# Finer steps at the sub-layer boundaries of a two-layer hybrid trunk: the last residual block in halves, and the second token tile's normalised blocks in a new order on ScalarE and VectorE

## The chip, the cores and the metric

The kernel runs on one core of one Trainium2 chip. A time is the device time of one execution in microseconds (us); lower is better. The kernel before took 1308.61 us, the median of 3 runs (1308.53 to 1309.16).

The core's engines each have an instruction queue that runs in order: PE (TensorE, the matrix engine), DVE (VectorE), ACT (ScalarE), POOL (GpSimd) and SP (SyncE, which issues most DMAs). An instruction can wait for a semaphore that another engine or a DMA raises; all that is queued behind it on its engine waits too.

## The reference, cut to what matters

256 tokens of width 1024 pass two layers. Each layer is an FFN, a mixer of four attention kinds, and a second FFN. Each sub-layer ends in a residual sum and a layer norm, and the next one begins with a modulation that is different in each:

```
for l in range(2):
    mod = (silu(c) @ ada_w[l] + ada_b[l]).reshape(-1, 3, 3, 1024)   # shift, scale, gate of each sub-layer
    h = 0.5 * swiglu(modulate(x, mod[0,0], mod[0,1]), w_in[l,0], w_out[l,0])
    x = layer_norm(ALPHA * x + (1 + mod[0,2]) * h, g[l,0], b[l,0])
    h = mixer(modulate(x, mod[1,0], mod[1,1]), ...)
    x = layer_norm(ALPHA * x + (1 + mod[1,2]) * h, g[l,1], b[l,1])
    h = 0.5 * swiglu(modulate(x, mod[2,0], mod[2,1]), w_in[l,1], w_out[l,1])
    x = layer_norm(ALPHA * x + (1 + mod[2,2]) * h, g[l,2], b[l,2])

modulate(x, shift, scale) = x * (1 + scale) + shift
swiglu(u, w_in, w_out)    = (silu(u @ w_in[:, :2816]) * (u @ w_in[:, 2816:])) @ w_out
```

## The kernel before, in words

**Split matmuls.** A float32 product is made of three matmuls. Each operand is split into a rounded high part (`hi`, made by ACT, line 262) and a low part that is the difference (`lo`, made by DVE, line 267); `split_mm` issues high by high, low by high and high by low (L286 to L288 where the weight is the stationary operand, L290 to L292 where the tokens are). The activations that a sub-layer reads are `uh` and `ul`, turned, with the width on the partitions; its weights stream in by DMA and are split as they come.

**Tiles.** The 256 tokens are two tiles, t=0 and t=1, of 128 partitions. A sub-layer's output is 2 x 1024 columns in four PSUM banks `accs`, each 128 x 512. In an FFN the hidden width of 2816 is 22 blocks of 128: `hidden(f)` makes one block, `post` its activation, `split_h` its two parts `hh` and `hl`, and `down` adds it to the four banks.

**The boundary.** There are five boundaries from one sub-layer to the next: FFN to mixer (first and fourth), mixer to FFN (second and fifth), FFN to FFN (third), and one end of the program. At each, the last matmuls run bank by bank in the order of `TAIL`, so the banks of t=0 end first and are normalised while PE is still at those of t=1. For each tile:
- `resid` (L401 to L403, DVE, one bank of 512 columns at a time): the sum times the gate row into `rt`, then ALPHA times x plus it, then `bn_stats`.
- `stats` (L406 and L407 on DVE, L408 on POOL): mean, variance, and the power -0.5 of it into `rstd`.
- `xhat` (four quarters q of 256 columns): normalised in place. The table `XA` says which quarters of each tile go to ACT (L416, with one small DVE instruction before them, L415); the rest go to DVE (L418). Before, tile 0 has two quarters on ACT and tile 1 none.
- `norm` (four quarters): PE turns two 128 x 128 blocks j into a PSUM bank (L426); ACT (L432) or DVE (L434) applies scale and shift into `utmp`; ACT casts it to `uh` (L436); DVE makes `ul = utmp - uh` (L437).

`GT` names, for each quarter of tile 0, behind which of the last matmuls its PE transposes are issued; `GF` and `GM` do so for tile 1, counted in contraction steps of the next sub-layer.

**What follows.** The next sub-layer's first matmuls use t=0 alone and run while t=1 is normalised: in an FFN the first two hidden blocks (a step kt of the contraction has two products, one of each block), in a mixer a piece of the V projection. Then the same matmuls run for t=1, in order of kt, so that quarter 0 is needed first. In an FFN, `h` of these first blocks stands with tokens on the partitions (L604, L605, L607) and is turned by PE (L609, `hT`) before it is split. Then `hidden(2)` and the rest follow. The affine part of the layer norm (`affine`, L485 and L486, four pieces of two DVE instructions) is needed only by the next residual sum and is issued in the hidden loop. A scheduler reorders by priority: work of a boundary is ahead (`tc.high_priority`), and `tc.issue_after(i)` holds an instruction behind another one in the order of issue.

## Time and profile before

| | |
|---|---|
| median of 3 runs | 1308.61 us |
| the profiled execution | 1315.82 us |
| its span (first to last instruction) | 1314.0 us |
| PE busy | 1265.7 us, 96% |
| DVE busy | 1036.5 us, 79% |
| ACT busy | 652.6 us, 50% |
| POOL busy | 142.8 us, 11% |
| granted TensorE clock | 0.998 of full speed |
| DMA, mean over the span | 229 GB/s |

A profile page sums a single execution of the program; it is 7.2 us longer than the median of the runs that were timed without a profile. Busy times of one engine can't be added to those of another, since the engines run beside each other. A row of the timeline gives the start and the duration of an instruction (or of `xN` that follow each other without a gap), and in brackets how long its engine had been idle and whose result ended that. Matmuls overlap: their pitch from start to start, not their duration, is the time that each costs PE. The places at which PE is idle are few, and those at the five boundaries are where the lines above meet.

### The profile page before, as it was taken

What the parts mean: (1) busy time and instruction counts of PE and PEld (TensorE: products, weight loads), DVE (VectorE), ACT (ScalarE), POOL (GpSimd) and SP (SyncE); (2) the same over time, 40 slices, a digit from 0 to 9 for tenths busy, and PEclk for the clock granted to TensorE, in tenths of its full rate; (3) what the DMA queues carried; (4) which work ended last, traced back from release to release, by engine and by line L of the source; (5) the groups of instructions that cost most, each with busy time, mean ns of one, the idle gap of its engine ahead of it and who ended that gap; (6) DMA issues with size and microseconds to landing.
All of it is one profiled execution on the core that took longest, in us unless ns stands there. A gap on an engine that the chain in (4) does not pass through costs nothing.

```text
span 1314.0 us, 23415 instructions
## 1 busy us (share of the span) xinstructions
PE 1265.7 (96%) x9178; PEld 1175.6 (89%) x9178; DVE 1036.5 (79%) x1701; ACT 652.6 (50%) x1023; POOL 142.8 (11%) x150
## 2 busy tenths in 40 slices
PE   6999999999999999999999999999999999999997
PEld 5989888989989889998989999899989898899995
DVE  7788887888786799877698877688878768976565
ACT  4554355447564554444355444354666545554440
POOL 0130000214222000000000000012060210100000
PEclk9999999999999999999999999999999999999999
DMA  9889893756665639887548987457476655585530
GB/s 341 324 285 313 302 306 141 255 185 223 225 235 181 227 127 319 302 277 262 175 147 312 311 282 248 128 171 239 163 248 232 222 182 175 215 315 193 187 135 33
DMA packets 85847, 300.42 MB, mean 229 GB/s; under 512 B 10604, under 2 KB 12316, under 8 KB 85736
## 3 DMA queue, kind: packets, MB, share of 16 engines
q1 hardware_dynamic: 84392, 298.00, 66.3%
q8 instruction: 72, 1.18, 0.4%
q10 hardware_dynamic: 576, 0.60, 0.1%
q0 software_dynamic: 768, 0.32, 0.1%
q14 instruction: 39, 0.32, 0.1%
HBM read 297.81 MB, written 1.07 MB: 227 GB/s over the span
## 4 chain that ended last, share of the span: by engine, by line
PE 43%; issue 19%; DMA 16%; DVE 15%; ACT 5%; POOL 1%; DVEq 0%; ACTq 0%; SPq 0%; POOLq 0%
PE mm L286 9%; PE mm L287 8%; PE mm L288 8%; DVE lo L267 6%; DMA raw<-in_w_in_dram 5%; DMA raw<-in_adac_dram 5%; PE acc L290 3%; PE acc L292 3%; PE acc L291 3%; ACT hi L262 3%; DMA raw<-in_w_out_dram 3%; DVE raw L308 3%; DMA raw<-in_mpair_dram 1%; PE tp L286 1%; PE mm L290 1%
## 5 line engine op out<-in xcount | busy, mean ns | idle before, releaser
L267 DVE TENSOR_TENSOR lo<-raw,hi 128x1024 fp32r<-128x1024 f32 (+2 forms) x421 | 508.1, 1222 | 161.3 <-ACT hi L262 159.2
L262 ACT CAST hi<-raw 128x1024 fp32r<-128x1024 f32 (+1 forms) x422 | 433.8, 1040 | 322.3 <-PE mm L287 126.9
L286 PE MATMUL mm<-uh,hi 128*128 128x256 f32 x2032 | 574.7, 283 | 5.3 <-DVE h L525 3.1
L287 PE MATMUL mm<-ul,hi 128*128 128x256 f32 x2032 | 571.2, 281 | 0.0
L288 PE MATMUL mm<-uh,lo 128*128 128x256 f32 x2032 | 570.6, 281 | 0.0
L286 PEld LDWEIGHTS mm<-uh,hi 128*128 128x128 f32 x2032 | 383.0, 189 | 12.2 <-issue 5.3
L287 PEld LDWEIGHTS mm<-ul,hi 128*128 128x128 f32 x2032 | 383.5, 189 | 1.3
L288 PEld LDWEIGHTS mm<-uh,lo 128*128 128x128 f32 x2032 | 383.1, 189 | 0.3
L308 DVE CUSTOM_DVE_ANT_0 raw<-raw,cond_row,adab 128x1024 f32<-128x1024 f32 x128 | 163.9, 1292 | 47.1 <-DMA raw<-in_adac_dram 47.0
L290 PE MATMUL acc<-hi,hh 128*128 128x512 f32 x352 | 140.6, 400 | 2.2 <-ACT hh L531 1.7
L291 PE MATMUL acc<-lo,hh 128*128 128x512 f32 x352 | 139.1, 395 | 0.8 <-DVE lo L267 0.8
L292 PE MATMUL acc<-hi,hl 128*128 128x512 f32 x352 | 137.6, 396 | 0.1
L290 PEld LDWEIGHTS acc<-hi,hh 128*128 128x128 f32 x352 | 66.1, 188 | 17.7 <-ACT hh L531 3.3
L531 ACT CAST hh<-h 128x256 fp32r<-128x256 f32 x82 | 33.2, 405 | 97.4 <-DVE h L525 95.7
L292 PEld LDWEIGHTS acc<-hi,hl 128*128 128x128 f32 x352 | 65.9, 187 | 17.1 <-DVE hl L532 0.6
L291 PEld LDWEIGHTS acc<-lo,hh 128*128 128x128 f32 x352 | 66.1, 188 | 15.0 <-DVE lo L267 1.1
L408 POOL TENSOR_TENSOR rstd<-rstd,nhalf 128x1 f32<-128x1 f32 x12 | 7.6, 634 | 479.8 <-DVE rstd L407 479.8
L532 DVE TENSOR_TENSOR hl<-h,hh 128x256 fp32r<-128x256 f32 x74 | 31.2, 421 | 12.6 <-ACT hh L531 12.6
L290 PE MATMUL acc<-hi,uh 128*128 128x256 f32 (+1 forms) x128 | 38.7, 303 | 1.5 <-ACT uh L436 1.4
L1073 POOL TENSOR_TENSOR merged<-merged,tg 128x512 f32<-128x512 f32 x16 | 24.8, 1548 | 135.7 <-DVE tg L1071 57.2
L286 PE MATMUL tp<-y,hi 128*128 128x256 f32 x112 | 33.2, 297 | 5.8 <-ACT pt L753 5.7
L292 PE MATMUL acc<-hi,ul 128*128 128x256 f32 (+1 forms) x128 | 38.3, 299 | 0.0
(242 smaller groups left out, 1519.7 us busy)
## 6 DMA issues: line engine op xcount, KB each, us to landing
raw<-in_w_in_dram SPq DMA_DIRECT2D x174, 512.0 KB, 5.5
raw<-in_adac_dram SPq DMA_DIRECT2D x128, 512.0 KB, 5.4
raw<-in_mpair_dram SPq DMA_DIRECT2D x104, 512.0 KB, 4.9
raw<-in_w_out_dram SPq DMA_DIRECT2D x88, 512.0 KB, 5.3
ada<-in_ada_dram SPq DMA_DIRECT2D x16, 512.0 KB, 6.7
raw<-in_mwo_dram SPq DMA_DIRECT2D x16, 512.0 KB, 4.5
raw<-in_mv_dram SPq DMA_DIRECT2D x16, 384.0 KB, 3.8
raw<-in_mbr_dram SPq DMA_DIRECT2D x12, 512.0 KB, 3.8
```

What stands on the lines that cost most here:

```text
L262: nc.scalar.copy(hi[:, :half], raw[:, :half])
L267: held["lo"] = nc.vector.tensor_sub(lo[:, :half], raw[:, :half], hi[:, :half].bitcast(F32)).ins
L286: nc.tensor.matmul(ps, lhsT=wh, rhs=xh, start=start, stop=False)
L287: nc.tensor.matmul(ps, lhsT=wh, rhs=xl, start=False, stop=False)
L288: nc.tensor.matmul(ps, lhsT=wl, rhs=xh, start=False, stop=stop)
L290: nc.tensor.matmul(ps, lhsT=xh, rhs=wh, start=start, stop=False)
L291: nc.tensor.matmul(ps, lhsT=xh, rhs=wl, start=False, stop=False)
L292: return nc.tensor.matmul(ps, lhsT=xl, rhs=wh, start=False, stop=stop).ins
L308: nc.vector.tensor_tensor_reduce(raw, raw, cond_row, 0.5, adab_sb[:, l * 3 + s, v, n:n + 1], ALU.mult, ALU.add, accum_out=t[:, n:n + 1])
L531: nc.scalar.copy(hh, h)
L532: eng.tensor_sub(hl, h, hh.bitcast(F32))
L1073: eng.tensor_tensor(mg, mg, t, op=ALU.add)
```

## The change

Seven edits, all at the boundaries:
1. The last bank, columns 512 to 1023 of t=1, is worked in two halves of 256 columns: its last matmuls are issued for columns 512 to 767 and then for 768 to 1023 (`TAIL`; `stop` is set on the second half alone), and `resid` takes it in two halves. `bn_stats` of t=1 is in groups of 256. `GT` is doubled, since the list of tail matmuls now counts halves; the places in time stay the same.
2. `XA`: quarters 2 and 3 of tile 1 are normalised on ACT.
3. `norm` of tile 1, quarter 0, is `direct`: ACT writes `uh` from the turned PSUM block itself (L442 after), DVE makes `utmp` from the same block (L446), and the cast is left out.
4. The other quarters of tile 1, and the tanh of the next FFN's first blocks, are issued after quarter 0.
5. The turn of `h` of the first two hidden blocks moves from behind each tile's matmuls to behind `hidden(2)`, and its split with it.
6. An `affine` piece is issued after the newest `lo` split.
7. The down projection of the first two blocks begins one hidden block later.

```diff
-XA = ((0,2),())
-GT = (3,3,2,1)
+XA = ((0,2),(2,3))
+GT = (6,6,4,2)
@@ boundary
-        def resid(t, h):
-            c = slice(h * 512, (h + 1) * 512)
-            nc.vector.tensor_tensor(rt[:, t, c], accs[t * 2 + h], G[:, c], op=ALU.mult)
+        groups = (512, 256)
+
+        def resid(t, c0, n):
+            c = slice(c0, c0 + n)
+            nc.vector.tensor_tensor(rt[:, t, c], accs[t * 2 + c0 // 512][:, c0 % 512:c0 % 512 + n], G[:, c], op=ALU.mult)
             nc.vector.scalar_tensor_tensor(xt[t][:, c], xt[t][:, c], ALPHA, rt[:, t, c], op0=ALU.mult, op1=ALU.add)
-            nc.vector.bn_stats(st6[:, 2 * t + h], xt[t][:, c])
+            for a in range(c0, c0 + n, groups[t]):
+                nc.vector.bn_stats(st6[:, 2 * t + a // groups[t]], xt[t][:, a:a + groups[t]])
...
-            for j in range(2):
-                src, sc, bi = ps[:, j * 128:(j + 1) * 128], gd[:, kt + j:kt + j + 1], bd[:, kt + j:kt + j + 1]
-                if on_act:
-                    nc.scalar.activation(tmp[:, j], src, AF.Identity, bias=bi, scale=sc)
-                else:
-                    nc.vector.tensor_scalar(tmp[:, j], src, sc, bi, op0=ALU.mult, op1=ALU.add)
-            uh = u[0][:, kt:kt + 2, t * 128:(t + 1) * 128]
-            ia = nc.scalar.copy(uh, tmp)
-            iv = nc.vector.tensor_sub(u[1][:, kt:kt + 2, t * 128:(t + 1) * 128], tmp, uh.bitcast(F32))
+            uh, ul = (z[:, kt:kt + 2, t * 128:(t + 1) * 128] for z in u)
+            direct = t == 1 and q == 0
+            with ExitStack() as order:
+                if t == 1 and q:
+                    for i in last["q0"]:
+                        order.enter_context(tc.issue_after(i))
+                for j in range(2):
+                    src, sc, bi = ps[:, j * 128:(j + 1) * 128], gd[:, kt + j:kt + j + 1], bd[:, kt + j:kt + j + 1]
+                    if direct:
+                        ia = nc.scalar.activation(uh[:, j], src, AF.Identity, bias=bi, scale=sc)
+                    if on_act and not direct:
+                        nc.scalar.activation(tmp[:, j], src, AF.Identity, bias=bi, scale=sc)
+                    else:
+                        nc.vector.tensor_scalar(tmp[:, j], src, sc, bi, op0=ALU.mult, op1=ALU.add)
+                if not direct:
+                    ia = nc.scalar.copy(uh, tmp)
+                iv = nc.vector.tensor_sub(ul, tmp, uh.bitcast(F32))
+            if direct:
+                last["q0"] = (ia.ins, iv.ins)
+                held["q0"] = ia.ins
...
-                resid(1, 1)
+                resid(1, 512, 256)
+                resid(1, 768, 256)
@@ ffn
-    TAIL = ((0, 0, 512), (0, 512, 512), (1, 0, 512), (1, 512, 512))
+    TAIL = ((0, 0, 512), (0, 512, 512), (1, 0, 512), (1, 512, 256), (1, 768, 256))
...
-                     hl[:, t * 128:(t + 1) * 128], f == 0, f == NF - 1, w_stationary=False)
+                     hl[:, t * 128:(t + 1) * 128], f == 0, f == NF - 1 and (n == 512 or c0 == 768), w_stationary=False)
...
-                nc.scalar.activation(th, ps[:, :, 0], AF.Tanh, scale=0.5)
+                with tc.issue_after(held["q0"]):
+                    nc.scalar.activation(th, ps[:, :, 0], AF.Tanh, scale=0.5)
...
-                for f in range(2):
-                    nc.tensor.transpose(hT[:, f, t], h[:, f], ident)
-            for f in range(2):
-                split_h(f, hT[:, f].rearrange("p a b -> p (a b)"))
+                h2.append(h)
+
+            def turn_h():
+
+                for t, h in enumerate(h2):
+                    for f in range(2):
+                        with tc.issue_after(held["pe"]):
+                            nc.tensor.transpose(hT[:, f, t], h[:, f], ident)
+                for f in range(2):
+                    split_h(f, hT[:, f].rearrange("p a b -> p (a b)"))
         for f in range(f0, NF):
             hidden(f)
+            if not first and f == f0:
+                turn_h()
             if not first and f >= AFF and held["affine"]:
-                held["affine"].pop(0)()
+                with tc.issue_after(held["lo"]):
+                    held["affine"].pop(0)()
...
-            while 2 * j + 1 < min(f, NF - tail) and n < MAXD:
+            while 2 * j + 1 < min(f - (f0 == 2 and f == 2), NF - tail) and n < MAXD:
```

`held["pe"]` is the last matmul of the newest `split_mm` with stationary weights. The mixer's output projection walks the same `TAIL`.

The order of issue on DVE from the end of the tail of the first boundary, FFN to mixer (`x_109` is tile 1; a bracket names the engines whose semaphores the instruction waits for). Before:

```order
L401 TENSOR_TENSOR rt<-acc,G 128x512 [waits PE_49]
L437 TENSOR_TENSOR ul<-utmp,uh 128x2x128 [waits Activation_49]
L402 SCALAR_TENSOR_TENSOR x_109<-x_109,rt 128x512 [waits DVE_49]
L437 TENSOR_TENSOR ul<-utmp,uh 128x2x128 [waits Activation_49]
L403 BN_STATS st_2246<-x_109 128x6 [waits DVE_49]
L406 BN_AGGR mvar<-st_2246 128x2 [waits DVE_49]
L407 TENSOR_SCALAR rstd<-mvar 128x1 [waits DVE_49]
L418 TENSOR_SCALAR x_109<-x_109,mvar,rstd 128x256 [waits Pool_49]
```


After:

```order
L404 TENSOR_TENSOR rt<-acc,G 128x256 [waits PE_49]
L404 TENSOR_TENSOR rt<-acc,G 128x256
L405 SCALAR_TENSOR_TENSOR x_109<-x_109,rt 128x256 [waits DVE_49] x2
L407 BN_STATS st_2261<-x_109 128x6 [waits DVE_49] x2
L449 TENSOR_TENSOR ul<-utmp,uh 128x2x128 [waits Activation_49]
L410 BN_AGGR mvar<-st_2261 128x2 [waits DVE_49]
L449 TENSOR_TENSOR ul<-utmp,uh 128x2x128 [waits Activation_49]
L411 TENSOR_SCALAR rstd<-mvar 128x1 [waits DVE_49]
L422 TENSOR_SCALAR x_109<-x_109,mvar,rstd 128x256 [waits Pool_49]
L422 TENSOR_SCALAR x_109<-x_109,mvar,rstd 128x256
L419 TENSOR_SCALAR sums<-mvar,rstd 128x1
L446 TENSOR_SCALAR utmp<-mm,gd,bd 128x128 [waits Activation_49] x2
```


The last block's three steps are now two of each, and both `rt` halves stand together: the first waits for PE, the second for nothing. Behind the power of POOL there are two `x` quarters where there were four, the small `sums` instruction, and the two `utmp` blocks of quarter 0, which wait for ACT.

The order on ACT at the same boundary, from the first instruction for tile 1's turned blocks. Before:

```order
L432 ACTIVATE utmp<-mm,bd,gd 128x128 [waits PE_49]
L432 ACTIVATE utmp<-mm,bd,gd 128x128
L730 COPY V<-acc 128x384 [waits PE_49]
L436 CAST uh<-utmp 128x2x128 [waits Activation_49]
L432 ACTIVATE utmp<-mm,bd,gd 128x128 [waits DVE_49,PE_49]
L436 CAST uh<-utmp 128x2x128 [waits DVE_49]
L432 ACTIVATE utmp<-mm,bd,gd 128x128
L436 CAST uh<-utmp 128x2x128 [waits Activation_49]
L436 CAST uh<-utmp 128x2x128 [waits DVE_49]
```


After:

```order
L420 ACTIVATE x_109<-x_109,sums,rstd 128x256 [waits DVE_49,Pool_49]
L420 ACTIVATE x_109<-x_109,sums,rstd 128x256
L442 ACTIVATE uh<-mm,bd,gd 128x128 [waits PE_49]
L759 COPY V<-acc 128x384 [waits PE_49]
L442 ACTIVATE uh<-mm,bd,gd 128x128 [waits DVE_49]
L444 ACTIVATE utmp<-mm,bd,gd 128x128 [waits PE_49]
L444 ACTIVATE utmp<-mm,bd,gd 128x128
L448 CAST uh<-utmp 128x2x128 [waits Activation_49]
L448 CAST uh<-utmp 128x2x128 [waits DVE_49] x2
```


Two quarters of `x` now stand ahead of the first block, and the two `uh` blocks (L442) are apart: the first waits for PE, the second for DVE, with the copy of V between them.

The order on DVE at the second boundary, mixer to FFN, from the last bank's first step (`x_108` is tile 0; L485 and L486 are the affine pieces before). Before:

```order
L401 TENSOR_TENSOR rt<-acc,G 128x512 [waits PE_49]
L437 TENSOR_TENSOR ul<-utmp,uh 128x2x128 [waits Activation_49] x2
L402 SCALAR_TENSOR_TENSOR x_109<-x_109,rt 128x512 [waits DVE_49]
L486 TENSOR_TENSOR x_108<-x_108,b 128x512
L403 BN_STATS st_5315<-x_109 128x6 [waits DVE_49]
L485 TENSOR_TENSOR x_108<-x_108,g 128x512
L406 BN_AGGR mvar<-st_5315 128x2 [waits DVE_49]
L486 TENSOR_TENSOR x_108<-x_108,b 128x512 [waits DVE_49]
L407 TENSOR_SCALAR rstd<-mvar 128x1 [waits DVE_49]
L418 TENSOR_SCALAR x_109<-x_109,mvar,rstd 128x256 [waits Pool_49]
```


After:

```order
L404 TENSOR_TENSOR rt<-acc,G 128x256 [waits PE_49]
L449 TENSOR_TENSOR ul<-utmp,uh 128x2x128 [waits Activation_49]
L405 SCALAR_TENSOR_TENSOR x_109<-x_109,rt 128x256 [waits DVE_49]
L449 TENSOR_TENSOR ul<-utmp,uh 128x2x128 [waits Activation_49]
L407 BN_STATS st_5351<-x_109 128x6 [waits DVE_49]
L404 TENSOR_TENSOR rt<-acc,G 128x256
L405 SCALAR_TENSOR_TENSOR x_109<-x_109,rt 128x256 [waits DVE_49]
L407 BN_STATS st_5351<-x_109 128x6 [waits DVE_49]
L410 BN_AGGR mvar<-st_5351 128x2 [waits DVE_49]
L411 TENSOR_SCALAR rstd<-mvar 128x1 [waits DVE_49]
L422 TENSOR_SCALAR x_109<-x_109,mvar,rstd 128x256 [waits Pool_49]
L422 TENSOR_SCALAR x_109<-x_109,mvar,rstd 128x256
```


The four affine instructions of tile 0 no longer stand between the last bank and the power; the second half's three steps stand behind the first half's.

## Rows read from the trace of the kernel before

**Rows 1.** The page: busy time, share of the span and instructions of each engine.

```profile
PE 1265.7 (96%) x9178; PEld 1175.6 (89%) x9178; DVE 1036.5 (79%) x1701; ACT 652.6 (50%) x1023; POOL 142.8 (11%) x150
```

**Rows 2.** What PE waited for (engine line, producer: us in all, times, longest us).

```profile
PE mm L426 <- DVE x L418: 3.9, 5, 1.0
PE mm L286 <- DVE h L525: 3.1, 3, 1.2
PE acc L290 <- ACT uh L436: 1.4, 4, 0.4
PE hT L609 <- DVE h L607: 1.1, 3, 0.5
```

**Rows 3.** Timeline, first boundary, FFN to mixer: start us, us, engine, line, operation, [idle].

```profile
205.22 0.21 DVE L415 TENSOR_SCALAR sums<-mvar,rstd 128x1 f32<-128x1 f32 x1 [0.70 <-POOL rstd L408]
205.47 1.09 ACT L416 ACTIVATE x<-x,sums,rstd 128x256 f32<-128x256 f32 x2 [0.78 <-DVE sums L415]
...
209.81 0.69 DVE L401 TENSOR_TENSOR rt<-acc,G 128x512 f32<-128x512 f32 x1
...
212.41 0.21 DVE L406 BATCH_NORM_AGGREGATE mvar<-st 128x2 f32<-128x12 f32 x1
...
212.88 0.56 POOL L408 TENSOR_TENSOR rstd<-rstd,nhalf 128x1 f32<-128x1 f32 x1 [1.37 <-DVE rstd L407]
213.48 1.38 DVE L418 TENSOR_SCALAR x<-x,mvar,rstd 128x256 f32<-128x256 f32 x4 [0.68 <-POOL rstd L408]
...
213.95 0.44 PE L426 MATMUL mm<-ident,x 128*128 128x128 f32 x2 [0.54 <-DVE x L418]
...
214.43 0.81 ACT L432 ACTIVATE utmp<-mm,bd,gd 128x128 f32<-128x128 f32 x2 [3.66 <-PE mm L426]
...
215.12 0.48 ACT L730 COPY V<-acc 128x384 f32<-128x384 f32 x1
...
215.48 0.42 ACT L436 CAST uh<-utmp 128x256 fp32r<-128x256 f32 x1
...
215.94 0.43 DVE L437 TENSOR_TENSOR ul<-utmp,uh 128x256 fp32r<-128x256 f32 x1
...
215.96 0.44 PE L290 MATMUL acc<-hi,uh 128*128 128x384 f32 x1 [0.38 <-ACT uh L436]
...
216.28 0.41 DVE L434 TENSOR_SCALAR utmp<-tp,gd,bd 128x128 f32<-128x128 f32 x1
216.42 0.44 PE L292 MATMUL acc<-hi,ul 128*128 128x384 f32 x1
...
217.56 0.33 PE L292 MATMUL acc<-hi,ul 128*128 128x384 f32 x1
```

**Rows 4.** Timeline, second boundary, mixer to FFN.

```profile
468.64 0.28 PE L290 MATMUL acc<-hi,uh 128*128 128x256 f32 x1
...
473.03 0.69 DVE L486 TENSOR_TENSOR x<-x,b 128x512 f32<-128x512 f32 x1
...
474.48 1.38 DVE L418 TENSOR_SCALAR x<-x,mvar,rstd 128x256 f32<-128x256 f32 x4 [0.69 <-POOL rstd L408]
...
474.94 0.44 PE L426 MATMUL mm<-ident,x 128*128 128x128 f32 x2 [0.96 <-DVE x L418]
...
476.85 0.38 PE L290 MATMUL acc<-hi,uh 128*128 128x256 f32 x1 [0.33 <-ACT uh L436]
...
477.35 0.39 PE L292 MATMUL acc<-hi,ul 128*128 128x256 f32 x1
```

**Rows 5.** Timeline, the end of the program.

```profile
1304.95 0.40 PE L291 MATMUL acc<-lo,hh 128*128 128x512 f32 x1
...
1305.18 0.39 PE L292 MATMUL acc<-hi,hl 128*128 128x512 f32 x1
1305.61 0.69 DVE L401 TENSOR_TENSOR rt<-acc,G 128x512 f32<-128x512 f32 x1 [2.52 <-PE acc L292]
...
1307.79 0.21 DVE L406 BATCH_NORM_AGGREGATE mvar<-st 128x2 f32<-128x12 f32 x1
```

More of the change, by code (lines that the diff above doesn't have):

```diff
@@ L233, in small_inputs @@
             nc.sync.dma_start(xt[t], x[t])
-    held = {"ins": [], "left": 0, "free": 0}
+    held = {"tail": [], "ins": [], "left": 0, "free": 0}
     def behind():
@@ L287, in split_mm @@
             nc.tensor.matmul(ps, lhsT=wh, rhs=xl, start=False, stop=False)
-            nc.tensor.matmul(ps, lhsT=wl, rhs=xh, start=False, stop=stop)
+            held["pe"] = nc.tensor.matmul(ps, lhsT=wl, rhs=xh, start=False, stop=stop).ins
         else:
@@ L391, in boundary @@
     def boundary(rt, accs, i, G, g, b, u, nxt):
-        st6 = sp.tile([P, 4, 6], F32, tag="st6", bufs=1, name="st6")
+        st6 = sp.tile([P, 6, 6], F32, tag="st6", bufs=1, name="st6")
         mv = [sp.tile([P, 2], F32, tag=f"mvar{t}", bufs=1, name="mvar") for t in range(2)]
@@ L397, in boundary @@
         last = {}
-        def resid(t, h):
-            c = slice(h * 512, (h + 1) * 512)
-            nc.vector.tensor_tensor(rt[:, t, c], accs[t * 2 + h], G[:, c], op=ALU.mult)
+        groups = (512, 256)
+        def resid(t, c0, n):
+            c = slice(c0, c0 + n)
+            nc.vector.tensor_tensor(rt[:, t, c], accs[t * 2 + c0 // 512][:, c0 % 512:c0 % 512 + n], G[:, c], op=ALU.mult)
             nc.vector.scalar_tensor_tensor(xt[t][:, c], xt[t][:, c], ALPHA, rt[:, t, c], op0=ALU.mult, op1=ALU.add)
-            nc.vector.bn_stats(st6[:, 2 * t + h], xt[t][:, c])
+            for a in range(c0, c0 + n, groups[t]):
+                nc.vector.bn_stats(st6[:, 2 * t + a // groups[t]], xt[t][:, a:a + groups[t]])
         def stats(t):
-            nc.vector.bn_aggr(mv[t], st6[:, 2 * t:2 * t + 2])
+            nc.vector.bn_aggr(mv[t], st6[:, 2 * t:2 * t + D // groups[t]])
             (nc.gpsimd if t in PA else nc.vector).tensor_scalar(rstd[t], mv[t][:, 1:2], EPS, None, op0=ALU.add)
@@ L453, in boundary @@
                 gdbd = next_mod(i, nxt)
-            resid(0, 0)
-            resid(0, 1)
+            resid(0, 0, 512)
+            resid(0, 512, 512)
             stats(0)
@@ L458, in boundary @@
                 store(0)
-                resid(1, 0)
-                resid(1, 1)
+                resid(1, 0, 512)
+                resid(1, 512, 256)
+                resid(1, 768, 256)
                 stats(1)
@@ L463, in boundary @@
                 return
-            resid(1, 0)
+            resid(1, 0, 512)
             for q in range(4):
@@ L473, in finish @@
             with tc.high_priority(offset=BP):
-                resid(1, 1)
+                resid(1, 512, 256)
+                resid(1, 768, 256)
                 stats(1)
@@ L590, in ffn @@
             hT = ptp.tile([P, 2, 2, 128], F32, tag="tp", name="hT")
+            h2 = []
             for t in range(2):
@@ L630, in ffn @@
         for f in range(2 * j, NF - tail):
-            for t, c0, n in TAIL:
-                down(f, t, c0, n)
+            for t in range(2):
+                for h in range(2):
+                    down(f, t, h * 512, 512)
         for t, c0, n in TAIL:
-            held["tail"] = [down(f, t, c0, n) for f in range(NF - tail, NF)]
+            held["tail"] = held["tail"] * (c0 == 768) + [down(f, t, c0, n) for f in range(NF - tail, NF)]
         boundary(rt, accs, i, G, grow, brow, nu, nxt)
@@ L1102, in out @@
             return split_mm(accs[t * 2 + c0 // 512][:, c0 % 512:c0 % 512 + n], ws[c](kk * D + c0, n),
-                            mh[:, kt, t * 128:(t + 1) * 128], ml[:, kt, t * 128:(t + 1) * 128], kt == 0, kt == KT - 1,
+                            mh[:, kt, t * 128:(t + 1) * 128], ml[:, kt, t * 128:(t + 1) * 128], kt == 0,
+                            kt == KT - 1 and (n == 512 or c0 == 768),
                             w_stationary=False)
         for kt in range(KT - TM):
-            for t, c0, n in TAIL:
-                out(kt, t, c0, n)
+            for t in range(2):
+                for h in range(2):
+                    out(kt, t, h * 512, 512)
         G, grow, brow = (mods[(l, 1)][k] for k in ("G", "g", "b"))
@@ L1112, in mixer @@
         for t, c0, n in TAIL:
-            held["tail"] = [out(kt, t, c0, n) for kt in range(KT - TM, KT)]
+            held["tail"] = held["tail"] * (c0 == 768) + [out(kt, t, c0, n) for kt in range(KT - TM, KT)]
         boundary(rt, accs, l * 3 + 1, G, grow, brow, nu, nxt)
```

## The prediction

> **What bounds the kernel now.** I read the page's busy times first. [...] Next the list of PE's waits, in which the boundaries have lines of their own: for the normalised `x` of tile 1, 3.9 us in 5 times; for `uh`, 1.4 in 4; for the turned `h`, 1.1 in 3; and just behind that turn for the bank that `h` of a hidden block frees, 3.1 in 3 [rows 2]. Everything that this change can win inside the program is about these 9.5 us. Then the timelines. At the first boundary [rows 3] the reader is to see a chain in which each link waits for the one ahead: last bank free, three DVE steps, aggregate, POOL power (ends at 213.44; I call this moment T), `x` on DVE, transposes on PE (213.95), two blocks on ACT, copy of V on ACT, cast, `ul`, PE. PE's first product with the new block starts 2.52 us behind T (215.96), the one that needs `ul` 2.98 (216.42), and the one that needs `ul` of quarter 1 4.12 (217.56). At the second boundary [rows 4] PE reaches the transposes at 474.94 - 0.96 = 473.98, behind 5.34 us of t=0 work that began at 468.64, and then waits for `x`.
>
> **The halved bank.** It would help if DVE could begin on columns 512 to 767 while PE is at 768 to 1023. The order of issue says that it can't: of the two `rt` halves at the first boundary the first waits for PE and the second for nothing, so that one wait already covers the last matmul of both. So the block starts when it did and is made of more instructions. A step of 512 takes 0.69 us, and on DVE steps that depend on each other start 0.73 apart, three of them in 2.18 [rows 5]; four quarters of 256 in a queue take 1.38, 0.345 each, and one alone 0.41 [rows 3]. Six halves cost between 6 x 0.345 = 2.07 and 6 x 0.41 = 2.46 us. At the end of the program the three steps took 1307.79 - 1305.61 = 2.18, so that place gives between -0.1 and +0.3; I take 0, since the halves alternate and can follow each other without a gap. At a mixer boundary there were 2.60 us from the first step to the aggregate (212.41 - 209.81), with two `ul` between; now one `ul` is between them, and one between aggregate and rstd: T moves by -0.1 to +0.4, I take +0.1. On PE a product of 512 columns costs 0.23 us (1305.18 - 1304.95 [rows 5]), and 45 of 256 fill the 5.34 us of t=0 work, 0.117 to 0.119 each: two are 0.003 to 0.007 dearer than one of 512. With 15 products at each boundary and 21 at the end, 96, I take the lower, +0.3 (bound +0.7).
>
> [...]
>
> **`x` quarters on ACT, and the direct block, at FFN to mixer (two places).** DVE makes quarters 0 and 1 (T+0.04 to T+0.73) and then `sums` (0.21, to T+0.94). ACT's pair of quarters is 1.09 us [rows 3], from T+0.98 to T+2.07, and in ACT's order it stands ahead of the first `uh` block. The transposed block is there at T+0.95 as before (214.39), so ACT is 1.1 us late for it. Then the two engines take turns, as the waits in the order say: ACT block 0 (T+2.1 to 2.5), DVE block 0 (0.41, to 2.95), on ACT beside it the copy of V (0.48, to 3.0), ACT block 1 (to 3.45), DVE block 1 (to 3.9), `ul` (0.43, to 4.4). The cast of 0.42 that goes was one link; what comes is two turns. PE's first product starts at T+2.55, as before; the one that needs `ul` at T+4.4 where it was T+2.98. With T's 0.1 this is 1.5 us late. Quarter 1 follows: its two blocks stand behind that `ul` on DVE, to T+5.1, cast to 5.5, `ul` to 6.0, so the product that had been at T+4.12 comes 1.9 + 0.1 = 2.0 late. Bounds: if `uh` and `ul` each released one block by itself, 1.0; if quarter 3 is late as well, 2.5. I take 1.9 each, **+3.8**.
>
> [...]
>
> **The same at mixer to FFN (two) and FFN to FFN (one).** Here the affine instructions go from between the last bank and the power; two of 0.69 stood right ahead of it [rows 4], so T comes 1.4 us earlier. But PE can't start the transposes before 473.98, so only the 0.96 wait goes. From there: block 0 on ACT to 474.85, the two `x` quarters to 475.95, block 1 to 476.4, DVE block 1 to 476.86, the `th` of the first hidden blocks (0.41), `ul` to 477.7. The product that needs it was at 477.35 [rows 4]: +0.35. Quarter 1, behind it on DVE and then in the cast, costs another 0.3, of which some is taken up by slack that PE had there. I take 0.4, 0.4 and 0.5, **+1.3** (bounds -1.0, the whole `x` wait won, and +0.8 each).
>
> **The turn of `h`, the affine pieces, the down projection.** Behind `hidden(2)` PE no longer waits for `h`: 1.1 us in three places goes [rows 2]. In return the `hh` and `hl` of the first two blocks stand behind those of block 2, and the first `lo` splits behind an adaLN reduction and, further on, the moved affine instructions. New waits of some 0.3 to 0.4 us at each of the three places are my estimate, so **0** in sum, with -4.2 (all waits of rows 2 for `h`, 3.1 + 1.1) and +3 as bounds.
>
> **Sum.** 3.8 + 1.3 + 0.3 + 0 + 0 = +5.4 us. On the profiled execution, 1315.82 becomes 1321.2; that run is 7.2 us above the median of the timed ones, and none of the terms depends on it, so the median becomes 1308.61 + 5.4 = **1314.0 us**, 0.4% slower.
>
> **Rivals.**
> - *The change does what it says.* The first half is read while PE works on the second, the direct block is two short links. Then three of six halves (1.05 us) lie beside PE at all six places, and the waits of PE for `x` and `uh`, 5.3 us [rows 2], go, with 1.1 for the turned `h` and 1.05 at the end: 1308.6 - 7.1 = 1301.5. For it: these waits are real and each in PE's way. Against it: the two `rt` halves with one wait, and the ACT order. It would take a trace in which the first `rt` half starts some 1.7 us before PE's last tail matmul.
> - *The FFN side pays for the mixer side.* DVE is 1.4 us ahead at three boundaries, and all waits for `h` go: +5.4 - 4.2 = +1.2, 1309.8, no difference that can be told. For it: 3.1 us of waits stand just behind the turn. Against it: the same DVE gets 8.3 us of affine work (3 x 4 x 0.69) back a little later.
> - *The moved affine work is what decides.* Those 8.3 us fall among the `lo` splits of the first hidden blocks. DVE is busy for 79% [rows 1]; if PE waits for each of them, 1308.6 + 5.4 + 8.3 = 1322.3. This begins where a `lo` is ready later than PE asks for its block; before, no wait of PE for a weight of an FFN's hidden blocks stands among the longest, so there is slack.
> - *A gain of a few us from FFN alone*, the mixer's loss being taken up by DVE and ACT work further on: -3 to -4, 1305. For it: attention has waits on ACT and DVE behind the projections. Against it: these begin with the projections' results and move with them.
>
> **How the numbers follow.** Forecast 0.60 (1311.5 to 1317.5 by its terms' bounds). FFN pays, or losses taken up to nothing: 0.20. As meant: 0.08. FFN gain alone: 0.06. Affine decides: 0.06. Of changes below 0.2%, 2.6 us, a measurement of this kernel can't tell much; the forecast's own bounds put 0.04 of its 0.60 inside that. So faster 0.14, same 0.24, slower 0.62. The range leaves out most of "as meant" and half of "affine decides": 1304.0 to 1318.5.
>
> **What would show it.** In the new profile: at both FFN-to-mixer boundaries ACT's two `x` quarters end before the first `uh` block starts, and four instructions alternate between ACT and DVE; PE's wait for `ul` is about 1.5 us there and a new line for `ul` of quarter 1 follows. The first `rt` half starts behind the last tail matmul, everywhere. At FFN boundaries PE's wait for `x` is gone and one for `ul` has come. It is wrong if the first `rt` half starts early, if PE's waits at the mixer boundaries sum to no more than before, or if FFN blocks 2 to 5 show waits for `lo` that outweigh all this.

## The result, and the profile after

The changed kernel took 1332.68 us, the median of 5 runs (1324.52 to 1334.39), against 1309.16 for the kernel before (5 runs): ratio 1.016, 95% interval 1.0133 to 1.0187: some 21 us slower by the ratio, 23.5 by the medians. The forecast had the sign (+5.4 us), but a quarter of the size, and the time lies above its range. The profiled execution took 1324.52 us, the shortest of the five, with a span of 1322.5 us. That span is 8.5 us above the one of before, so the rows below show less than half of what the medians lose.

From the page of the changed kernel, as in [rows 1]; then PE's waits, as in [rows 2] (engine line, producer: us, times, longest us):

```profile
PE 1265.8 (96%) x9274; PEld 1174.3 (89%) x9274; DVE 1039.7 (79%) x1730; ACT 657.9 (50%) x1028; POOL 143.0 (11%) x150
```

```profile
PE acc L290 <- ACT hh L548: 9.4, 12, 1.4
PE mm L286 <- DVE h L542: 7.4, 6, 2.0
PE acc L292 <- DVE ul L449: 4.8, 5, 1.2
...
PE acc L292 <- DVE hl L549: 1.4, 4, 0.4
PE mm L430 <- ACT x L420: 1.4, 3, 0.5
```

PE's busy time is what it was, so what this execution has more is, by the page, idle time of PE. The wait of tile 1's `x` on DVE (3.9 us before) is gone but for 1.4 us that ACT now causes; 4.8 us of waits for `ul` have come. These are the boundary. The large new waits are elsewhere: for `hh` 9.4 us where it was 1.7 (in the same list of before, a single wait), for the bank that `h` frees 7.4 where it was 3.1 [rows 2], and 1.4 for `hl`. They lie in the FFNs.

The first boundary in the timeline (start us, us, engine, line, operation, [idle]) answers to [rows 3]:

```profile
209.90 0.56 POOL L412 TENSOR_TENSOR rstd<-rstd,nhalf 128x1 f32<-128x1 f32 x1 [1.24 <-DVE rstd L411]
...
210.50 0.74 DVE L422 TENSOR_SCALAR x<-x,mvar,rstd 128x256 f32<-128x256 f32 x2 [0.68 <-POOL rstd L412]
...
211.45 1.09 ACT L420 ACTIVATE x<-x,sums,rstd 128x256 f32<-128x256 f32 x2 [3.65 <-DVE sums L419]
...
212.45 0.44 ACT L442 ACTIVATE uh<-mm,bd,gd 128x128 fp32r<-128x128 f32 x1
...
212.92 0.41 DVE L446 TENSOR_SCALAR utmp<-mm,gd,bd 128x128 f32<-128x128 f32 x1 [1.57 <-ACT uh L442]
...
213.37 0.46 ACT L442 ACTIVATE uh<-mm,bd,gd 128x128 fp32r<-128x128 f32 x1
...
213.86 0.41 DVE L446 TENSOR_SCALAR utmp<-mm,gd,bd 128x128 f32<-128x128 f32 x1 [0.53 <-ACT uh L442]
214.31 0.42 DVE L449 TENSOR_TENSOR ul<-utmp,uh 128x256 fp32r<-128x256 f32 x1
...
214.78 0.44 PE L292 MATMUL acc<-hi,ul 128*128 128x384 f32 x1 [1.23 <-DVE ul L449]
...
216.40 0.44 PE L292 MATMUL acc<-hi,ul 128*128 128x384 f32 x1
...
217.25 0.52 PE L292 MATMUL acc<-hi,ul 128*128 128x384 f32 x1
...
217.57 0.52 PE L290 MATMUL acc<-hi,uh 128*128 128x384 f32 x1
```

T, the end of the power for tile 1 as in the prediction, is 210.46 here. The order is the predicted one, link by link: ACT's `x` pair until T+2.1, then ACT, DVE, ACT, DVE, `ul`, and PE's product at T+4.32 (forecast T+4.4); the third of quarter 1 at T+5.94 (forecast T+6.0). What was not forecast follows it. Windows of the same stretch (from:to, length, then busy time and instructions of PE, PEld, DVE, ACT, POOL; then the granted clock, the DMA share and GB/s):

```profile
213.00:214.00 1.00, 0.56 (x3) 0.24 (x2) 0.47 (x2) 0.88 (x3) 0.00 (x0) 1.00 0.00 0
214.00:215.00 1.00, 0.22 (x1) 0.22 (x2) 0.96 (x4) 0.93 (x3) 0.00 (x0) 1.00 0.00 0
...
216.00:217.00 1.00, 1.00 (x5) 0.76 (x6) 1.00 (x4) 0.95 (x2) 0.00 (x0) 0.87 0.00 0
217.00:218.00 1.00, 1.00 (x5) 1.00 (x4) 0.58 (x2) 1.00 (x2) 0.00 (x0) 0.50 0.00 0
...
220.00:221.00 1.00, 1.00 (x8) 1.00 (x7) 1.00 (x2) 0.24 (x1) 0.00 (x0) 0.92 0.89 303
```

PE was busy for 0.56 and 0.22 us of two successive microseconds while it waited; at about 216.7 its granted clock fell from 1.00 to 0.50 and stayed there until about 220.2. Two 384 products are 0.32 us apart there (217.57 - 217.25), where they were 0.17 apart before (216.87 - 216.70 in its timeline). Ten of them cost 1.5 us more, on top of the wait.

The second boundary's FFN in the changed kernel, some 20 us behind the power, and in the last row its longest wait:

```profile
490.33 2.35 DVE L267 TENSOR_TENSOR lo<-raw,hi 128x1024 fp32r<-128x1024 f32 x2
490.44 1.47 SPq L259 DMA_DIRECT2D raw<-in_w_out_dram  x2
...
492.61 0.41 DVE L542 SCALAR_TENSOR_TENSOR h<-th,mm 128x256 f32<-128x256 f32 x1
...
492.94 0.68 DVE L502 TENSOR_TENSOR x<-x,g 128x512 f32<-128x512 f32 x1
...
493.17 0.35 PE L286 MATMUL mm<-uh,hi 128*128 128x256 f32 x1 [0.74 <-DVE h L542]
...
493.88 0.68 DVE L503 TENSOR_TENSOR x<-x,b 128x512 f32<-128x512 f32 x1
...
496.40 1.05 ACT L262 CAST hi<-raw 128x1024 fp32r<-128x1024 f32 x1 [2.67 <-DMA raw<-in_w_out_dram]
...
497.36 0.37 ACT L548 CAST hh<-hT 128x256 fp32r<-128x256 f32 x1
...
497.77 0.50 PE L290 MATMUL acc<-hi,hh 128*128 128x512 f32 x1 [0.92 <-ACT hh L548]
...
607.66 0.38 PE L286 MATMUL mm<-uh,hi 128*128 128x256 f32 x1 [2.04 <-DVE h L542]
```

The reader is to see `h` of a hidden block (L542) behind two `lo` splits, and an affine pair (L502, L503) behind it. ACT then stands still for 2.67 us, since the weight that it is to split next hasn't landed, and `hh` of the turned blocks, queued behind that split on ACT, comes 0.92 us late for PE. The pair shown isn't what makes either late: `h` stands ahead of it, and SyncE issued the transfer of that weight at 490.44. Nor do all new waits lie near the boundary. The longest, 2.04 us at 607.66, comes 137 us behind T, where this boundary's last affine instruction starts 52 us behind the start of the power; four waits of 0.85 to 2.04 us at 125 to 137 us behind the second and third boundary's T sum to 6.1 us, where the kernel before has 1.9.

### The profile page after: what moved, and what is told of

It reads as the page before. It is cut to its first block, busy times and chain, and to the rows that moved or that the text cites. A ratio compares the mean times of both kernels' runs of the same rounds, so it can differ in the third digit from the quotient of the medians.

```text
span 1322.5 us, 23649 instructions
## 1 busy us (share of the span) xinstructions
PE 1265.8 (96%) x9274; PEld 1174.3 (89%) x9274; DVE 1039.7 (79%) x1730; ACT 657.9 (50%) x1028; POOL 143.0 (11%) x150
## 4 chain that ended last, share of the span: by engine, by line
PE 49%; DMA 20%; DVE 17%; issue 6%; ACT 6%; POOL 0%; DVEq 0%; ACTq 0%; SPq 0%
PE mm L286 10%; PE mm L287 10%; PE mm L288 10%; DMA raw<-in_w_in_dram 9%; DVE lo L267 7%; DMA raw<-in_adac_dram 6%; PE acc L292 4%; PE acc L290 4%; PE acc L291 4%; DMA raw<-in_w_out_dram 4%; ACT hi L262 4%; DVE raw L308 3%; PE mm L290 1%; PE tp L286 1%; PE mm L291 1%
## 5 line engine op out<-in xcount | busy, mean ns | idle before, releaser
L290 PE MATMUL acc<-hi,hh 128*128 128x512 f32 (+1 forms) x374 | 145.0, 388 | 9.4 <-ACT hh L548 9.4
L291 PE MATMUL acc<-lo,hh 128*128 128x512 f32 (+1 forms) x374 | 143.0, 382 | 0.5 <-DVE lo L267 0.5
L292 PE MATMUL acc<-hi,hl 128*128 128x512 f32 (+1 forms) x374 | 141.6, 384 | 1.8 <-DVE hl L549 1.4
L290 PEld LDWEIGHTS acc<-hi,hh 128*128 128x128 f32 x374 | 70.2, 188 | 26.8 <-ACT hh L548 13.9
L292 PEld LDWEIGHTS acc<-hi,hl 128*128 128x128 f32 x374 | 69.8, 188 | 19.6 <-DVE hl L549 4.9
L291 PEld LDWEIGHTS acc<-lo,hh 128*128 128x128 f32 x374 | 70.3, 188 | 13.9 <-DVE lo L267 0.8
L291 PE MATMUL acc<-lo,uh 128*128 128x256 f32 (+1 forms) x128 | 38.6, 302 | 0.0
```

Of the source, the lines that this page charges most:

```text
L290: nc.tensor.matmul(ps, lhsT=xh, rhs=wh, start=start, stop=False)
L291: nc.tensor.matmul(ps, lhsT=xh, rhs=wl, start=False, stop=False)
L292: return nc.tensor.matmul(ps, lhsT=xl, rhs=wh, start=False, stop=stop).ins
```

## The experiments

Each time below was measured beside runs of the kernel before on the same chip (its median there 1310.58 to 1311.98 us); the signed number is the difference of medians, and the ratio has its 95% interval (an expectation that quotes +3.8 for e2 or +8.9 for e8, or +2.7 for the sum of e1 and e6, went by the ratio). Granted clocks are means over a kernel's runs; the kernel before had 0.997 to 0.998.

### The parts alone, and the whole again

The whole change taken apart by its edits; each kernel has only the edits named, the rest as before.

```diff
 # e1: edit 1 (TAIL, resid, bn_stats, GT)       # e2: edits 2 to 4       # e3: edits 5 to 7
-    TAIL = ((0, 0, 512), (0, 512, 512), (1, 0, 512), (1, 512, 512))
+    TAIL = ((0, 0, 512), (0, 512, 512), (1, 0, 512), (1, 512, 256), (1, 768, 256))
```

> The kernel before with edit 1 alone (last bank in halves, bn_stats of tile 1 in 256 columns). Both theories: no early start of the first half, so about no change, -0.5 to +1.5 us; the first rt half starts behind the last tail matmul at all six places. If the halves did free the bank early, -2 us or more and a first rt half some 1.7 us before the last tail matmul.

Measured 1308.31 us, -2.3, ratio 0.9981 (0.9966 to 0.9996). No early start, as said, here at the end of the program:

```profile
1301.43 0.28 PE L292 MATMUL acc<-hi,hl 128*128 128x256 f32 x1
1301.74 0.75 DVE L404 TENSOR_TENSOR rt<-acc,G 128x256 f32<-128x256 f32 x2 [2.54 <-PE acc L292]
...
1303.86 0.26 DVE L410 BATCH_NORM_AGGREGATE mvar<-st 128x2 f32<-128x24 f32 x1
```

The first half's `rt` starts 0.31 us behind the start of the last tail matmul and 0.03 behind its end, with the second right behind it, and the three steps take 2.12 us where they took 2.18 [rows 5]. The small gain isn't explained by this.

> The kernel before with edits 2 to 4 alone (quarters 2 and 3 of tile 1 on ACT, direct first block, order behind it). Theory A, the forecast's (the direct block is what decides): +10 us or more of the measured +16 to +24 here, with the wait of PE for ul of about 1.2 us at both FFN-to-mixer boundaries and a stretch at the lower clock level behind it. Theory B (the turn of h and what goes with it decides): +3 to +8 us here, the rest elsewhere.

Measured 1313.47, +2.9, ratio 1.0029 (1.0011 to 1.0048): theory A is wrong.

> The kernel before with edits 5 to 7 alone (turn of h behind hidden(2), affine behind the lo split, down projection one block later). Theory A: 0, at most +3 us. Theory B: +8 us or more, with PE waiting for hh some 9 us in place of 1.7 and for h of hidden blocks some 7 in place of 3.1, in the first FFN blocks behind each of three boundaries.

Measured 1317.63, +7.1, ratio 1.0054 (1.0036 to 1.0073): most of what a part alone costs, in the part that the forecast had put at nothing. At the second boundary itself this kernel gains: by the pitch of the matmuls PE loses 0.6 us where it lost 2.6. Behind it more is lost.

> The changed kernel unchanged, on the chip of the other runs: +16 to +24 us over before by either theory. If edits add up, the sum of the three single ones; if the clock is what decides, more than the sum, since waits that are short each would fall together.

Measured 1330.52, +19.9, ratio 1.0135 (1.0107 to 1.0163), clock 0.994. The parts sum to +7.7: together the edits cost far more than apart.

> Edits 3 and 4 without the quarters on ACT: only the direct block and the order behind it. If the taking of turns is most of the +3.8 us of edits 2 to 4: +2 to +4 with PE's wait for ul still there. If the two x quarters ahead on ACT are: -1 to +1.5, and the wait for ul shorter than 0.5 us.

Measured 1311.52, 0.0, ratio 1.0004 (0.9986 to 1.0023), with waits for `ul` of 5.3 us in all, 1.2 the longest. Neither case held: the turn-taking is there, and it costs nothing that can be told, though the interval reaches +3.0. The intervals of e2 and e12 overlap, so whether the +2.9 of e2 belongs to the quarters isn't shown.

### Which of edits 5 to 7

> Edit 6 alone: affine pieces behind the newest lo. Theory C: what edits 5 to 7 win at a boundary comes from this one, and what they lose behind it comes from the turn and the down projection: -3 to -6 us, PE's wait for x at the three boundaries into an FFN about gone, no new wait for hh. Rival (the fourth rival of the forecast, moved affine work delays the lo splits): +3 us or more, PE waits for lo or h in the first hidden blocks.

```diff
-                held["affine"].pop(0)()
+                with tc.issue_after(held["lo"]):
+                    held["affine"].pop(0)()
```

Measured 1315.51, +4.2, ratio 1.0038 (1.0021 to 1.0056): theory C is wrong. DVE and PE in this kernel, some 47 us behind the power:

```profile
515.84 0.68 DVE L497 TENSOR_TENSOR x<-x,g 128x512 f32<-128x512 f32 x1
...
517.98 0.68 DVE L498 TENSOR_TENSOR x<-x,b 128x512 f32<-128x512 f32 x1
...
518.91 1.28 DVE L308 CUSTOM_DVE_ANT_0 raw<-raw,cond_row,adab 128x1024 f32<-128x1024 f32 x1
...
520.08 1.05 ACT L262 CAST hi<-raw 128x1024 fp32r<-128x1024 f32 x1 [0.65 <-DMA raw<-in_w_in_dram]
...
520.12 2.35 DVE L267 TENSOR_TENSOR lo<-raw,hi 128x1024 fp32r<-128x1024 f32 x2
...
522.39 0.41 DVE L544 TENSOR_TENSOR hl<-h,hh 128x256 fp32r<-128x256 f32 x1
...
522.86 0.50 PE L292 MATMUL acc<-hi,hl 128*128 128x512 f32 x1 [1.08 <-DVE hl L544]
```

An affine pair, two reductions and two `lo` splits stand ahead of `hl`, for which PE waits 1.08 us. What keeps `hl` back last is the second split, which needs the `hi` that ACT ends at 521.13; its weight was issued at 514.39, ahead of the pair. Without the pair, and in the same order, `hl` would come only some 0.1 us sooner by these rows. Waits for `hl` are 5.9 us in all here; before there is no such line among the waits.

> Edits 5 and 7 without 6. Theory C: +8 to +13 us, more than edits 5 to 7 together (+7.1), with the waits for hh and h in the FFN. Rival: near 0, and edit 6 has the loss.

Measured 1308.73, -2.6, ratio 0.9976 (0.996 to 0.9993). So the turn of `h` with the later down projection is harmless alone, and edit 6 has the loss.

> Edits 1 and 6 without the others, a candidate for a version better than both. If the two add: -2.3 (edit 1 measured) and -3 to -6, so -5 to -8 us, under 1306. If both win the same wait for x, -3 to -5.

Measured 1319.59, +8.3, ratio 1.0068 (1.0042 to 1.0093): a miss. The halves, -2.3 alone, seem to cost some 4 us in the company of edit 6, but the two intervals overlap, and in the company of edits 5 to 7 they gain 2.6 (e16, below, against e3).

> Edits 2 to 7, without the halved bank. The single parts were +3.8 (quarters and direct block) and +7.1 us (turn, affine, down). If they add: +11. If the quarters and the direct block also take back what the moved affine work wins at the three boundaries into an FFN (PE's lost time there fell from 2.6 to 0.6 us in the kernel with edits 5 to 7 alone, and is 2.5 in the changed kernel), +15 to +19, near the whole change, and the halves are no part of it.

Measured 1324.23, +12.9, ratio 1.0104 (1.0082 to 1.0127): about the sum of e2 and e3 plus 3.

> Edits 1, 5, 6 and 7, all without the quarters and the direct block. Sum of the single ones: -2.3 + 7.1 = +5. Edit 6 with the halves was +8.9 where their sum was +2.7, so by that pair +8 to +12, and the quarters and the direct block have the remaining +8 to +10 of the changed kernel. If it is under +5, the interplay needs the direct block.

Measured 1316.49, +4.5, ratio 1.003 (1.0016 to 1.0044), the sum of e1 and e3. Edits 2 to 4 on top of this make the changed kernel, so there they cost some 15 us, where alone they cost 3.

> Edits 1, 5 and 7: the three that were not slower alone, a candidate for a version better than both. If they add: -2.3 - 2.6 = about -5 us. If the halves and the turn want the same slack on VectorE: -2 to -3.

Measured 1311.01, -0.5, ratio 0.9995 (0.9973 to 1.0017): no version better than before.

### Work, or place

> The kernel before, with four more VectorE instructions of 128x512 (tile 0 times 1.0) in each FFN behind a boundary, in hidden blocks 3 and 4 behind the newest lo, where edit 6 puts four affine ones; the affine stays where it was. They are 3 x 4 x 0.69 = 8.3 us of work. Theory D: +5 to +10 us with waits for hl, h and hh in those FFNs. If VectorE had slack there and edit 6 costs by the order alone: 0 to +2.

```diff
                 held["affine"].pop(0)()
+                if f < AFF + 2:
+                    with tc.issue_after(held["lo"]):
+                        for h in range(2):
+                            hs = slice(h * 512, (h + 1) * 512)
+                            nc.vector.tensor_scalar(xt[0][:, hs], xt[0][:, hs], 1.0, None, op0=ALU.mult)
```

Measured 1304.27, -7.2, ratio 0.9947 (0.9929 to 0.9964): more work on DVE, and faster. The added instructions took 0.42 us, not 0.69, but the main point is another: they made the scheduler order the affine anew, with two of the four instructions gone from ahead of the power to between it and the first `lo`. So the place was the next thing to try.

> The kernel before, with each affine piece issued behind the last x quarter that VectorE makes of tile 1 (in edit 6 it is behind the newest lo). Two of the four instructions that stood ahead of the power now stand between x and utmp, where VectorE waits for PE's transposes; fewer go among the lo splits than in edit 6. Theory E (what counts is the place: ahead of the power costs the wait for x, among the lo splits costs hl and hh later, the wait for the transposes is free): -4 to -7 us, as with the extra VectorE work. Rival (the gain of that run came from another order further on): -1 to +2.

```diff
-                nc.vector.tensor_scalar(xt[t][:, hs], xt[t][:, hs], mv[t][:, 0:1], rstd[t], ...)
+                held["xh"] = nc.vector.tensor_scalar(xt[t][:, hs], xt[t][:, hs], mv[t][:, 0:1], rstd[t], ...).ins
...
-                held["affine"].pop(0)()
+                with tc.issue_after(held["xh"]):
+                    held["affine"].pop(0)()
```

Measured 1305.57, **-6.4**, ratio 0.9949 (0.9932 to 0.9965), in the range that theory E gave: with e11 the fastest, and better than both kernels. DVE at the second boundary, and PE's waits:

```profile
466.02 1.38 DVE L422 TENSOR_SCALAR x<-x,mvar,rstd 128x256 f32<-128x256 f32 x4 [0.69 <-POOL rstd L412]
467.32 1.29 DVE L497 TENSOR_TENSOR x<-x,g 128x512 f32<-128x512 f32 x2
468.52 0.73 DVE L443 TENSOR_SCALAR utmp<-tp,gd,bd 128x128 f32<-128x128 f32 x2
```

```profile
PE mm L286 <- DVE h L537: 2.1, 3, 0.8
...
PE acc L290 <- ACT hh L543: 1.6, 3, 0.9
PE acc L292 <- DVE ul L446: 1.4, 3, 0.5
...
PE mm L430 <- DVE x L422: 1.0, 2, 0.5
```

The power is early, as with edit 6, and two affine instructions stand between the `x` quarters and `utmp`. That place isn't free: waits for `ul` of 1.4 us have come. But the wait for `x` fell from 3.9 us to 1.0, and those for `h` and `hh` are 2.1 and 1.6 us, no longer than before [rows 2].

> The changed kernel with that placing of the affine pieces in place of edit 6. Theory E: the direct block has VectorE wait in just the stretch in which the affine pieces would be free, so at most half of the +18 to +20 goes: +7 to +12. Rival (edit 6 alone is to blame): +0 to +4.

Measured 1316.35, +4.4, ratio 1.0037 (1.0021 to 1.0052). Of the +19.9 of the changed kernel 15.5 go with this request alone (12.8 by the ratios).

> Edit 1 with the affine pieces behind the x quarters. With edit 6 in its place the halves gave +8.9. Theory E (place of the affine work): near -6.4 - 2.3 = -8, at least no slower than -4. If the halves spoil any early affine placing: 0 or more.

Measured 1313.66, +2.5, ratio 1.0022 (1.0003 to 1.004): a miss, and a telling one. DVE at the second boundary:

```profile
471.63 1.38 DVE L422 TENSOR_SCALAR x<-x,mvar,rstd 128x256 f32<-128x256 f32 x4 [1.17 <-POOL rstd L412]
...
476.45 0.68 DVE L499 TENSOR_TENSOR x<-x,g 128x512 f32<-128x512 f32 x1
477.05 5.76 DVE L267 TENSOR_TENSOR lo<-raw,hi 128x1024 fp32r<-128x1024 f32 x5
```

The same request for a place put nothing between `x` and `utmp` this time; the first affine instruction comes 4.8 us behind the `x` quarters' start, right ahead of the first `lo`, and the rest among the splits.

> Edits 1, 5 and 7 with the affine pieces behind the x quarters; with edits 2 to 4 on top this is the +4.4 us run. If the quarters and the direct block cost their own +3.8 here too: about 0. If they cost more where VectorE is early (they take the gain back): -4 to -9, so that they are worth 8 us or more.

Measured 1315.65, +4.5, ratio 1.0032 (1.0019 to 1.0044), as much as with the direct block (e14): again with none between `x` and `utmp`.

How many of the eight affine instructions of the second boundary start more than 7 us behind the start of its power, counted in each profile's timeline, against the time:

| kernel | late ones | us |
|---|---|---|
| before | 3 | 0 |
| e1 halves | 3 | -2.3 |
| e7 turn, down | 4 | -2.6 |
| e9 halves, turn, down | 4 | -0.5 |
| e11 extra work | 4 | -7.2 |
| e13 behind `x` | 6 | -6.4 |
| e17 halves, behind `x` | 7 | +2.5 |
| e18 halves, turn, behind `x` | 7 | +4.5 |
| e6 affine | 8 | +4.2 |
| e16 halves, turn, affine | 8 | +4.5 |
| e3 turn, affine | 8 | +7.1 |
| e8 halves, affine | 8 | +8.3 |

All of these have tile 1's quarters on DVE and no direct block. None with 6 or fewer is slower than before, all with 7 or 8 are. The bound of 7 us was chosen with the times known, and in the kernels with a direct block the count tells little: e12, e2 and e10 have 2 late ones each, at 0.0, +2.9 and +8.8, and e14 has 5, at +4.4.

Where in the program the affine's place costs time can be read from the ends of tile 1's powers, T at each boundary (us, one profiled execution each):

| profile | start to the first T | two stretches with a mixer | three with an FFN | span |
|---|---|---|---|---|
| before | 213.4 | 523.2 | 577.4 | 1314.0 |
| changed | 210.5 | 519.8 | 592.2 | 1322.5 |
| changed, second profile (e4) | 210.3 | 520.9 | 592.4 | 1323.6 |
| changed, affine behind `x` (e14) | 212.2 | 521.4 | 583.2 | 1316.9 |
| e6 affine | 212.5 | 515.2 | 585.6 | 1313.3 |
| e13 behind `x` | 208.4 | 515.6 | 575.4 | 1299.4 |

What the changed kernel loses lies in the FFN stretches, 15 us, and there e13 lies 10.2 below e6, and e14 9 below the changed kernel. The first column holds nearly the same work in all six, and differs by up to 5 us.

### The clock

> The changed kernel without edit 6. Theory D (the affine work moved among the lo splits is what decides, also in the interplay): the +18 to +20 of the changed kernel falls to about the sum of the other parts, -2.3 + 3.8 - 2.6, so -2 to +3 us. Rival (the quarters and the direct block with the turn are what multiplies, whatever the affine does): +10 or more stays.

Measured 1320.25, +8.8, ratio 1.0076 (1.0053 to 1.0098): neither case. Only two affine instructions are late here, but the mean clock is 0.991, the lowest of all. Windows in the FFNs behind the second, third and fifth boundary:

```profile
480.00:485.00 5.00, 4.67 (x22) 4.67 (x23) 5.00 (x12) 2.72 (x6) 0.00 (x0) 0.50 0.00 0
...
675.00:680.00 5.00, 5.00 (x36) 5.00 (x36) 5.00 (x9) 3.96 (x5) 0.00 (x0) 0.79 0.33 101
1125.00:1130.00 5.00, 4.07 (x22) 3.63 (x23) 5.00 (x15) 4.36 (x10) 0.00 (x0) 0.77 0.01 3
```

> The changed kernel without edit 6 (+8.8 us, granted clock 0.990 in its profile, lower level for some us behind all three boundaries into an FFN), with nine transposes of the identity on PE ahead of the first t=1 product at each boundary; their result is overwritten. They are 9 x 0.105 = 0.95 us where PE else waits up to 1.2 us for ul. If the falls of the clock are the price: they go at those places, and the time falls by 3 to 7 us although PE has more to do. If the waits alone are: 0 to +4 us more.

```diff
+    def fill(at, t):
+        for _ in range(9 * t):
+            nc.tensor.transpose(at, ident, ident)
...
+                    fill(ps[:, 0, 0], t)      # ahead of the first products of the hidden blocks; alike in the mixer
```

Measured 1319.54, +7.6, ratio 1.0053 (1.0034 to 1.0072), clock 0.9957. The same windows:

```profile
475.00:480.00 5.00, 4.95 (x29) 4.71 (x29) 5.00 (x14) 3.82 (x9) 0.00 (x0) 0.66 0.00 0
480.00:485.00 5.00, 5.00 (x45) 5.00 (x44) 4.90 (x6) 3.34 (x4) 0.00 (x0) 1.00 0.60 179
...
675.00:680.00 5.00, 5.00 (x45) 5.00 (x44) 5.00 (x7) 3.81 (x5) 0.00 (x0) 1.00 0.35 116
1125.00:1130.00 5.00, 3.97 (x32) 3.33 (x31) 3.89 (x12) 2.44 (x7) 0.72 (x2) 1.00 0.03 7
```

In this execution the fall is gone from these windows at the third and fifth boundary and shorter at the second; others have come at 687 to 691, in the FFN behind the third, and at 1110 to 1114, ahead of the fifth. Over all executions the filling raised the clock: five of e10's six lie at 0.989 to 0.991, all six of e15's at 0.993 to 0.997.

What the falls cost is another matter. A lower mean clock by 0.0063 (0.9973 - 0.991) would be 0.0063 x 1312 = 8.3 us of PE's work, as much as e10 loses. This count, the lost share of the mean clock times the time, is the author's estimate from the granted clocks above; in e10's profile the 256 products were 0.21 us apart at 0.50 (480.71 to 480.92), where those of the kernel before are 0.12 apart. e10's own executions speak against that price: the sixth had a mean clock of 0.997, that of the kernel before, and took 1320.28 us, as long as the five others (1320.03 to 1323.02). In the profiled execution's window at 480 to 485 DVE is busy for all of the 5.00 us, so PE's pace need not have been what counted there. In the kernel before the count fits better: over its 121 executions beside the runs, 0.001 less of clock goes with 1.2 us more, where the count gives 1.3. For e15 the count would be 6.2 us given back (0.0047) for 5 x 0.95 = 4.8 us of filling, part of it in the waits; the 0.95 is the expectation's estimate, and at the second boundary the nine took 1.76 us, from their start to that of the next product (477.36 - 475.60). By the differences e15 lost 1.2 us less than e10, with intervals that overlap. So the mean clock was 0.0047 higher with the filling, and nothing is shown of what that is worth. Why e10 costs 8.8 us is open.

## Why the prediction was wrong

- **The step that failed**: the turn of `h`, the affine pieces, the down projection. It said "New waits of some 0.3 to 0.4 us at each of the three places are my estimate, so **0** in sum". Edits 5 to 7 alone cost 7.1 us, edit 6 alone 4.2, edits 5 and 7 alone gain 2.6. In the changed kernel the waits for `hh`, `h` and `hl` are 13.4 us longer than before (9.4 + 7.4 + 1.4 - 1.7 - 3.1). The rival that "the moved affine work is what decides", 1322.3 us, named this place and had 0.06. Its reason, the amount of work, was not right: e6 and e13 have the same affine work and differ by 10.6 us, and e11 adds work there and gains. It looked for waits for `lo`, and so did the last sign under "What would show it"; PE's only such wait among the changed kernel's matmuls is 0.5 us.
- **What stands in its place**: the place of the affine instructions. e6 and e13, and the changed kernel and e14, differ in this request alone, and the time by 10.6 and 15.5 us, in the FFN stretches by the table above. Ahead of the power the affine delays T (at the second boundary it is 5.6 us behind the end of the last tail matmul before, 3.9 in e6 and e13), between `x` and `utmp` it costs least, behind the `lo` splits most. By which path is not shown. In the three FFN stretches ACT stands idle for weights that haven't landed for 88.8 us before, 126.5 and 125.0 in the two profiles of the changed kernel and 129.1 in e6, but 96.3 in e13 and 106.0 in e14; so the weights come later for ACT with edit 6, and `hh` stands behind their splits. But e11, the fastest, has 107.4, and at the two places read row by row the affine pair itself was not what `h`, `hh` or `hl` waited for.
- **A reading that was wrong**: the bank that `h` of a hidden block frees. The prediction, and the rival by which the FFN pays, put its 3.1 us of waits [rows 2] "just behind" the turn. In the trace of before they start at 172.37 us, in the first FFN, which has no boundary ahead of it, and at 604.60 and 796.89, 130 and 129 us behind T; the turn is 15 us behind it. So they were not the turn's to win, and -4.2 was no bound of this term.
- **The second step**: the sum counts each microsecond by which PE's products come later as one of the program. As a rule for a sum it was not borne out. In e12, `ul` waits of 5.3 us cost nothing that can be told; what took them up was not read. In the changed kernel the granted clock fell behind the boundary's waits, and ten products at 0.50 cost 1.5 us more; the sum had no term for that. Its mean clock was 0.9942 against 0.9977 (e4), 4.6 us of the 19.9 by the count, an estimate. Over its 11 executions the time rises as the clock falls, from 1321.80 and 1324.52 us at 0.996 to 1334.39 at 0.992, more than the count gives; whether the falls lengthen the time or longer waits bring the falls isn't shown, and e10 warns against taking the clock for the cause.
- **The halved bank**: no early start, as forecast. Its price, +0.3 for PE and 0.1 for T, was -2.3 as measured; why it gains is open.
- **Quarters and direct block**: forecast +5.1, alone +2.9 (1.4 to 6.3 by the ratio's interval). The chain at the mixer boundary was right to some 0.1 us in each link. That ACT's quarters and the alternating reads make one chain out of two engines' work is shown by the rows; that this is what costs is not (e12). At the boundaries into an FFN T came 0.8 to 1.0 us earlier behind the end of the last tail matmul (5.5 to 5.7 us before, 4.7 after), not 1.4.
- **The sums**: the stated range did not hold its own terms. Taken at their upper bounds together (5.0 + 2.4 + 0.7 + 3) they give +11.1, 1319.7 us, above 1318.5, and the measured time lies above that too. The rival "as meant" names 5.3, 1.1 and 1.05 us, 7.45 in sum, and takes off 7.1.
- **Edits do not add.** A sum of terms, each worked out against the order of before, was the wrong form: the scheduler orders DVE and ACT anew for each set of edits, and with the halves in, the same affine request lands elsewhere (e13 against e17). Of the +19.9, 15.5 depend on the affine's place (e14); the clock's share by the count overlaps with that. Why edits 2 to 4 cost some 15 us beside edits 1 and 5 to 7 (e16 against e4), and 0 where the affine is behind `x` (e18 against e14), is settled no further than that.

## What to carry to other kernels

Work that a scheduler may place is not priced by its duration but by where it is put: find the stretch in which it delays least and hold the work there, and look at the order again after every other edit. Where one engine is busy for 96%, look behind each new wait for a fall of the granted clock (in the changed kernel to 0.50 for some 3.5 us, behind a wait of 1.23). A share lost of the mean clock is an estimate of what it costs, not a measurement: compare executions of one kernel that differ in it, as e10's do, before it is called the cause. Read where in the program a wait stands before it is put down to a nearby step. Time edits alone and together before a sum over them is believed.
